# Q and K blocks of an encoder layer: fewer VectorE steps per block, and parts of Q, K and the gates emitted sooner

## The chip, the cores and the metric

The kernel runs on 1 core of one Trainium2 chip, as a single launch. The metric is the device time of that launch in microseconds (us). A core has one TensorE (PE), which multiplies matrices, and VectorE (DVE), ScalarE (ACT), GpSimd (POOL) and SyncE (SP), each with an instruction queue of its own that is worked off in order. The engines wait for each other through semaphores.

## The reference, cut to what matters

One encoder layer on a sequence of 1024 tokens of width 1024, fp32 in and out:

```python
u = rms_norm(x, norm1_g)
proj = u @ w_in                 # q | k | v | cb | cc | ch | ga | gb
q = rms_norm(q.reshape(B, S, 8, 64), q_norm_g)   # per head
k = rms_norm(k.reshape(B, S, 8, 64), k_norm_g)
y_a = neighbourhood_attention(q, k, v, rpb) @ w_attn_branch
y_b = short_gated_conv(cb, cc, ch, conv_w) @ w_conv_branch
merged = sigmoid(ga) * y_a + sigmoid(gb) * y_b
x = x + merged @ w_o
x = x + square(relu(rms_norm(x, norm2_g) @ w_mlp_in)) @ w_mlp_out

def rms_norm(x, g):
    return x * rsqrt(mean(x * x, axis=-1) + EPS) * g
```

q, k and v are 512 wide, and so are the convolution's cb, cc and ch; the gates ga and gb are 1024 wide each. The change touches the norm of q and k and what is emitted around it.

## The kernel before, in words

**Precision.** TensorE multiplies in fp16, with every fp32 operand split into a high part (its fp16 copy) and a low part (the value less that copy). Three passes (high by high, high by low, low by high) make up a product. A product of 1024 deep is therefore 24 matmuls of 128x128 by 128x512. The function `unit` emits these and adds one to a counter of units.

**Weights.** A piece of weights (the class `Chunk`) is loaded as raw fp32 in four parts by SyncE. Its `prep` squares the parts on ScalarE (L266), adds the sums on VectorE (L270, L272), adds over the partitions with a matmul by ones (L201), and from that makes a power of two as the scale. Then ScalarE writes the high parts (L306) and VectorE the low parts (L297). After each pair of low parts, SyncE is given the next load (`load_upto`): there are five raw buffers.

**Order.** The order of instructions on each engine is written out by hand, as the order of emission. Work beside the matmuls stands in Python generators of which every `yield` ends a step. Those in `fg` are advanced by `step`, those in `bg` (weights, first come first served) by `tick`. `unit(mms, post, steps, ticks)` emits a product, then what was put off until the product was emitted, and then so many steps and ticks. A generator that has to stand back until a unit count is reached does so by `apart`.

**The stage of the change.** After norm 1 (`norm`; ScalarE, GpSimd and VectorE) and its transposes by DMA (`turn_row`), the V units follow, then eight units of Q (rows in the order 2, 6, 3, 7, 4, 5, 0, 1), eight units of K, the first chunk of the convolution in two halves, and then the attention. Beside the Q units also run: `sforms`, which turns rows of the normed input into the gates' sums and differences (rows scaled on ScalarE at L484, four GpSimd instructions per pair of rows at L490, high and low parts at L504 and L506, and a store). Its table SFORM gives at which unit count which pair is scaled and summed (last number 0) or split into its parts (1). K's weight parts are made beside the Q units, and those of the first convolution chunk beside the K units.

**One block of Q or K** (`qk_vec`): ScalarE moves the product out of its PSUM bank (L714, which is also when the bank is free) and squares it (L715). VectorE sums per head (L718). `rstd` makes the inverse root: a VectorE step that adds epsilon (L405), the root on ScalarE (L406), then four VectorE steps (L408 to L414) that refine it. K's result is then scaled once more (L722). VectorE multiplies the block by it (L725), and for K by the norm weights (L728). ScalarE copies the high part (L732) and VectorE writes the low part (L734). For Q both parts are written twice side by side (1024 wide). The result stands in one of two buffers, and `finish_qk`, three units later, transposes it by a DMA on SyncE's queue (L745). Q and K units take PSUM banks "d" and "o" by turns; there are three banks "d", three "s" and two "o". Both halves of the first convolution chunk take banks "o" (L794). The loop emits

```python
        unit(tok_mms(ps, actU, b, ch, 8, 512, 0), post, 4, 6 if 4 < n < 8 else 3)
```

that is, four steps and three or six ticks per block.

Of the kernel before, what the change touches and what calls it, by code (L numbers as in the profile page):

```python
# [21 lines left out]
HD = 64  # L22
# [30 lines left out]
def encoder_block(ctx: ExitStack, tc: tile.TileContext, x, weights, cols, gqk, rel, masks, out):  # L53
# [22 lines left out]
        return bank("dsodsods"[rc[0] % 8])  # L76


    sc = base.tile([128, 516], F32, name="sc")
    sci = sc.bitcast(I32)  # L80
    area = {"keep": [0, 0, 148], "prep": [148, 148, 244], "tmp": [244, 244, 516]}

    def cols_of(kind, n):
        a = area[kind]
# [6 lines left out]
    def keep(n=1):  # L91
        return cols_of("keep", n)

    def tmp(n=1):
        return cols_of("tmp", n)

    def at(c, i, n=1):
        return slice(c.start + i, c.start + i + n)

    def mul(a, b, out=None):  # L100
        out = out or tmp(a.stop - a.start)
        V.tensor_tensor(sc[:, out], sc[:, a], sc[:, b], op=OP.mult)
        return out
# [78 lines left out]
    def apart(mark, n=3, of=units):  # L182
        while of[0] < mark + n and not forced[0]:
            yield WAIT
# [37 lines left out]
    def settle():  # L222
        while late:
            late.pop(0)()
# [20 lines left out]
    class Chunk:  # L245
# [9 lines left out]
        def prep(self):  # L255
            n = len(self.widths)
            nk = sum(k for k, _ in self.widths)
            rm, a, b, s = (cols_of("prep", i) for i in (nk, 1, 1, 1))
            self.inv = keep()
            tot = sum(k * w for k, w in self.widths)  # L260
            if self.kind in "QKCG":
                self.parts = wsp.tile([128, 2, tot], F16, name="w16_ws", tag="ws")
                for p, (k, w) in enumerate(self.widths):
                    while len(self.raw) <= p:
                        yield WAIT
                    A.activation(self.parts[:, 1, :k * w].bitcast(BF16), self.raw[p][:, :k * w], AF.Square,  # L266
                                 accum_out=sc[:, at(rm, p)])
                    spend(0, 300 + k * w * 7 // 8)
                    yield
                V.tensor_reduce(sc[:, a], sc[:, at(rm, 0, n)], axis=AX, op=OP.add)  # L270
                c = ones_col()
                V.tensor_tensor(c, sc[:, a], sc[:, gm2], op=OP.mult)  # L272
                yield from apart(units[0], 1 if self.kind == "Q" else 3)
                yield from all_sum(c, b, bank(self.bank) if self.bank else anybank(), 1e-36, int(self.kind != "Q"))
                yield from pow2_half(b, 14, s, self.inv, more=self.more)
            else:
                yield from self.largest(rm, a, b)
                yield from pow2(b, 14, s, self.inv, False, more=self.more)
            V.tensor_scalar(sc[:, rm], sc[:, self.rows], sc[:, s], None, op0=OP.mult)  # L279
            yield  # L280
            while done[0] < self.first or self.tag not in wpool:
                yield WAIT
            if self.kind not in "QKCG":
                self.parts = wpool[self.tag].tile([128, 2, tot], F16, name="w16_" + self.tag, tag=self.tag)
            f = o = 0
            todo = []
            for p, (k, w) in enumerate(self.widths):
                todo.append((p, [(i * w, w, rm.start + o + i) for i in range(k)], f))
                f += k * w
                o += k  # L290
            prev = None
            for it in todo + [None]:
                if prev:
                    p, parts, f = prev
                    for o, m, c in parts:
                        hi, lo = (self.parts[:, w, f + o:f + o + m] for w in range(2))
                        V.scalar_tensor_tensor(lo, self.raw[p][:, o:o + m], sc[:, c:c + 1], hi,  # L297
                                               op0=OP.mult, op1=OP.subtract)
                    done[0] += 1
                    load_upto(done[0] + 5)  # L300
                    spend(sum(m + 130 for _, m, _ in parts))
                if it:
                    p, parts, f = it
                    spend(0, sum(m * 7 // 8 + 120 for _, m, _ in parts))
                    for o, m, c in parts:
                        A.activation(self.parts[:, 0, f + o:f + o + m], self.raw[p][:, o:o + m], AF.Copy,  # L306
                                     scale=sc[:, c:c + 1])
                prev = it
                self.split = it is None
                yield  # L310
# [81 lines left out]
    def gain(g, top, s, inv):  # L392
# [5 lines left out]
        yield  # L398
        yield from pow2(m, top, s, inv, floor=False)

    def rstd(ss, n, y, top):

        k = ss.stop - ss.start
        v, q = tmp(k), tmp(k)
        V.tensor_scalar(sc[:, v], sc[:, ss], 4.0 ** -top / n, 4.0 ** -top * EPS, op0=OP.mult, op1=OP.add)  # L405
        A.activation(sc[:, q], sc[:, v], AF.Sqrt)  # L406
        yield
        V.reciprocal(sc[:, y], sc[:, q])  # L408
        yield
        V.scalar_tensor_tensor(sc[:, q], sc[:, y], -0.5, sc[:, y], op0=OP.mult, op1=OP.mult)  # L410
        yield
        mul(q, v, q)
        yield
        V.scalar_tensor_tensor(sc[:, y], sc[:, q], 1.5, sc[:, y], op0=OP.add, op1=OP.mult)  # L414
        yield
# [20 lines left out]
    def norm(xin, sq, u, y, pool):  # L436

        ss = tmp()
        A.activation(sq, xin, AF.Square, accum_out=sc[:, ss])
        yield  # L440
        yield from rpow(ss, D, y, 9)
        if pool:
            G.tensor_scalar(u[:, 0], xin, sc[:, y], 1.0, op0=OP.mult, op1=OP.mult)
        else:
            A.activation(u[:, 0], xin, AF.Copy, scale=sc[:, y])
        yield
        V.scalar_tensor_tensor(u[:, 1], xin, sc[:, y], u[:, 0], op0=OP.mult, op1=OP.subtract)
# [25 lines left out]
    ys = keep(8)  # L473
    ORDER, BYPOOL = (2, 6, 3, 7, 4, 5, 0, 1), (4, 5)
    ln = [norm(xt[:, b], sq, u16[:, ORDER.index(b) % 4], at(ys, b), b in BYPOOL) for b in range(8)]
    GS = dram.tile([128, 4, 4, 2, 512], F16, name="gs")

    turned, formed = set(), [0]
    SFORM = ((9, 0, 0), (9, 2, 1), (10, 1, 0), (10, 3, 1), (11, 0, 1), (12, 1, 1))

    def sform_rows(n):
        assert n in turned and n + 4 in turned
# [31 lines left out]
    def ln_step(b, n=1):  # L514
        for _ in range(n):
            advance(ln[b])

    def qk_gain():
        g = gq[:, 0]
        V.tensor_tensor(g, g, gq[:, 1], op=OP.mult)  # L520
        yield
        yield from gain(g, 11, sgq, isgq)

    def turn_row(b):
        ln_turn(u16[:, ORDER.index(b) % 4], b, UT)
# [145 lines left out]
                v_post(b, j, s)  # L671
    v_unit(2, 0)
    settle()
    for b in 4, 5:
        ln_step(b)
        turn_row(b)
# [3 lines left out]
    tick(2)  # L680
    v_unit(6, 0)
    settle()
    tick()
    v_unit(3, 0)
    sform_rows(3)
    sform_sums(3)
    tick(2)
    v_unit(7, 1)
    for b in 0, 1:
        ln_step(b, 2)  # L690
        turn_row(b)
    fg.append(qk_gain())
    fg.append(sforms())
    for b in 4, 5:
        v_unit(b, 11)
# [15 lines left out]
    def qk_vec(ps, inv, kind, res):  # L711
        qs = wqk.tile([128, 512], F32, name="qs", bufs=3)
        sq = wqk.tile([128, 512], F32, name="sq", bufs=1)
        A.activation(qs, ps, AF.Copy, scale=sc[:, inv])  # L714
        A.activation(sq, qs, AF.Square)  # L715
        yield
        ss, y = tmp(8), tmp(8)
        V.tensor_reduce(sc[:, ss], sq.rearrange("p (h d) -> p h d", h=8), axis=AX, op=OP.add)  # L718
        yield
        yield from rstd(ss, HD, y, 12 if kind == "q" else 0)  # L720
        if kind == "k":
            V.tensor_scalar(sc[:, y], sc[:, y], sc[:, sgq], None, op0=OP.mult)  # L722
            yield
        q3 = qs.rearrange("p (h d) -> p h d", h=8)
        V.tensor_tensor(q3, q3, sc[:, y][:, :, None].to_broadcast([128, 8, HD]), op=OP.mult)  # L725
        yield
        if kind == "k":
            V.tensor_tensor(q3, q3, gq[:, 0][:, None, :].to_broadcast([128, 8, HD]), op=OP.mult)  # L728
        r = 2 if kind == "q" else 1
        t = wqk.tile([128, 8, 2, r, HD], F16, name=kind + "16", tag="q16")  # L730
        q4 = q3[:, :, None, :].to_broadcast([128, 8, r, HD])
        A.activation(t[:, :, 0], q4, AF.Copy)  # L732
        yield
        V.tensor_tensor(t[:, :, 1], q4, t[:, :, 0], op=OP.subtract)  # L734
        res.append(t)

    q16 = {}
# [9 lines left out]
    for n, (kind, b) in enumerate(todo):  # L747
# [5 lines left out]

        def post(ps=ps, kind=kind, n=n, ch=ch):
            fg.append(qk_vec(ps, ch.inv, kind, q16[n]))
        unit(tok_mms(ps, actU, b, ch, 8, 512, 0), post, 4, 6 if 4 < n < 8 else 3)
        if n == 3:
            forced[0] = True
            while formed[0] < 4:
# [31 lines left out]

    conv_start(0)
    push(cConv[1])
    first = [bank("o"), bank("o")]  # L794
    for half in range(2):
        unit(ch_mms(first[half], actU, half, cConv[0], 8, 384, 0), None, 8, 4)
        finish_qk(13 + half)
# [1124 lines left out]
```

## Time and profile before

| | before |
|---|---|
| time, median of 3 runs | 1205.65 us (1205.05 to 1205.97) |
| the profiled execution: its time | 1205.96 us |
| the profiled execution: its span | 1204.2 us |
| granted TensorE clock | 1.0 |
| PE busy | 1190.9 us (99%) |
| DVE busy | 929.0 us (77%) |
| ACT busy | 763.3 us (63%) |
| POOL busy | 435.1 us (36%) |

The span is what the profile shows from the first to the last instruction; the time of that execution is 1.8 us more. A row of a timeline begins with the start in us from the beginning of the span, then the length, the engine, the line of the program, the operation and what it writes and reads; in brackets stand the idle time ahead of it and who ended that. Rows of grouped lines give, after the shapes and the count, the busy time in us, the mean of one in ns, and the idle time ahead of them.

### The profile page before, as it was taken

The page shows a single profiled execution, that of the slowest core. Times are in us where ns is not written, and L with a number is a line of the kernel's source. Part 1 is how long each engine was busy: PE and PEld are TensorE (multiplying, and loading weights), DVE is VectorE, ACT ScalarE, POOL GpSimd, SP SyncE. Part 2 cuts the span into 40 slices and gives each one's busy share as a digit, 9 for nine tenths or more (in the row PEclk, how much of TensorE's full clock was granted, in tenths as well). Part 3 has the DMA queues.
Part 4 walks back from the last instruction along what each step waited for, and adds up shares of the span by engine and source line. Part 5 has one row for each costly group of instructions (what it writes and reads, how often), then busy time and mean ns, then how long its engine had stood idle before and what let it go on. Part 6 is the DMA issues. An engine that isn't in the chain of part 4 may idle for free.

```text
span 1204.2 us, 16886 instructions
## 1 busy us (share of the span) xinstructions
PE 1190.9 (99%) x6206; PEld 574.7 (48%) x6206; DVE 929.0 (77%) x1721; ACT 763.3 (63%) x1185; POOL 435.1 (36%) x292
## 2 busy tenths in 40 slices
PE   8999999999999999999999999999999999999998
PEld 6444445555444444444468444444444444444444
DVE  6767988988368686877878655545549999999997
ACT  7876679867554555337779778678676744746440
POOL 1641011222311112001004465565567471554662
PEclk9999999999999999999999999999999999999999
DMA  9956746676451211224286545445465926345302
GB/s 284 220 181 139 139 119 134 130 146 120 106 121 68 64 60 52 70 92 188 53 159 185 183 156 192 151 138 193 147 247 201 355 94 223 124 139 194 105 35 105
DMA packets 177250, 174.91 MB, mean 145 GB/s; under 512 B 137744, under 2 KB 138256, under 8 KB 173072
## 3 DMA queue, kind: packets, MB, share of 16 engines
q1 hardware_dynamic: 176592, 169.65, 49.0%
q10 hardware_dynamic: 576, 4.19, 0.8%
q8 instruction: 48, 0.79, 0.3%
q14 instruction: 34, 0.28, 0.1%
HBM read 102.51 MB, written 37.75 MB: 116 GB/s over the span
## 4 chain that ended last, share of the span: by engine, by line
PE 78%; DVE 5%; issue 1%; SPq 1%; ACT 1%; DMA 0%; DVEq 0%; ACTq 0%
PE ps_d L210 28%; PE ps_s L210 24%; PE ps_o L210 17%; PE ps_d L1017 6%; PE ps_o L994 1%; PE ps_s L937 1%; SPq L1088 1%; DVE P L977 1%; DVE w_s L1141 1%; DVE sz L951 1%; DVE sg L1257 0%; DVE w_ws L297 0%; ACT w_s L1145 0%; DMA uT<-gs 0%; DVE sc L317 0%
## 5 line engine op out<-in xcount | busy, mean ns | idle before, releaser
L210 PEld LDWEIGHTS <-ops 128*128 128x128 f16 x1356 | 132.5, 98 | 157.3
L210 PEld LDWEIGHTS <-w 128*128 128x128 f16 x1368 | 132.9, 98 | 139.4
L1017 PE MATMUL ps_d<-uT,w_ws 128*128 128x512 f16 x528 | 123.7, 379 | 0.1
L210 PE MATMUL ps_d<-ops 128*128 128x512 f16 (+1 forms) x528 | 118.3, 374 | 0.0
L1743 ACT ACTIVATE ops<-hf,sc 128x2048 f16<-128x2048 f32 x26 | 52.0, 2000 | 98.2 <-PE ps_o L210 35.5
L210 PE MATMUL ps_s<-ops 128*128 128x512 f16 x492 | 112.9, 379 | 0.0
L1130 POOL TENSOR_TENSOR tsum<-raw 128x512 f32<-128x512 f32 x28 | 46.3, 1668 | 148.8 <-ACT raw L1116 148.7
L1323 POOL TENSOR_TENSOR as<-as 128x512 f32<-128x512 f32 x56 | 77.5, 1385 | 38.9 <-ACT as L1603 35.6
L210 PEld LDWEIGHTS <-w_s 128*128 128x128 f16 x588 | 56.7, 98 | 69.6 <-DVE w_s L1141 1.5
L210 PEld LDWEIGHTS <-uT 128*128 128x128 f16 x528 | 51.4, 98 | 64.0 <-issue 2.3
L210 PE MATMUL ps_d<-u2x,w 128*128 128x512 f16 (+1 forms) x360 | 80.0, 372 | 0.0
L1017 PEld LDWEIGHTS <-w_ws 128*128 128x128 f16 x528 | 51.2, 98 | 54.5 <-DVE cv L839 0.4
L210 PE MATMUL ps_o<-ops 128*128 128x512 f16 x336 | 77.1, 379 | 0.0
L1745 DVE SCALAR_TENSOR_TENSOR ops<-hf,sc,ops 128x2048 f16<-128x2048 f32 x26 | 73.4, 2822 | 4.3 <-ACT ops L1743 4.2
L210 PE MATMUL ps_o<-u2T,w 128*128 128x512 f16 (+1 forms) x324 | 71.7, 371 | 0.0
L1116 ACT ACTIVATE raw<-raw,sc 128x256 f32<-128x256 f32 x172 | 71.0, 494 | 0.9 <-DMA raw<-in_weights 0.9
L1130 POOL TENSOR_TENSOR gsum<-raw 128x512 f32<-128x512 f32 x14 | 19.0, 1377 | 132.3 <-issue 71.3
L1145 ACT ACTIVATE w<-raw,sc 128x512 f16<-128x512 f32 (+1 forms) x28 | 24.6, 927 | 54.0 <-DVE sc L432 54.0
L210 PE MATMUL ps_s<-u2T,w 128*128 128x512 f16 (+1 forms) x252 | 52.7, 359 | 0.0
L1636 DVE TENSOR_TENSOR as<-ps_d,as 128x512 f32<-128x512 f32 (+1 forms) x14 | 9.4, 672 | 55.7 <-ACT as L1655 53.4
L960 ACT ACTIVATE sz<-sz,sc 128x384 f32<-128x384 f32 (+1 forms) x64 | 37.2, 582 | 22.4 <-DVE sc L951 15.0
L306 ACT ACTIVATE w_ws<-raw,sc 128x512 f16<-128x512 f32 (+2 forms) x72 | 40.8, 637 | 14.2 <-DVE sc L279 14.2
(360 smaller groups left out, 2633.5 us busy)
## 6 DMA issues: line engine op xcount, KB each, us to landing
raw<-in_weights SPq DMA_DIRECT2D x88, 512.0 KB, 5.3
hs<-as SPq DMA_DIRECT2D x16, 1792.0 KB, 8.8
hf<-hs SPq DMA_DIRECT2D x26, 1024.0 KB, 7.4
w2x<-in_weights SPq DMA_DIRECT2D x16, 512.0 KB, 8.6
raw<-in_weights SPq DMA_DIRECT2D x16, 384.0 KB, 3.4
xt<-in_x SPq DMA_DIRECT2D x8, 512.0 KB, 8.1
gs<-s ACTq DMA_DIRECT2D x4, 1024.0 KB, 3.9
x<-in_x SPq DMA_DIRECT2D x8, 512.0 KB, 10.1
```

The source lines that it names most:

```text
L210: T.matmul(ps, l, r, start=a, stop=b)
L306: A.activation(self.parts[:, 0, f + o:f + o + m], self.raw[p][:, o:o + m], AF.Copy, scale=sc[:, c:c + 1])
L937: T.matmul(ps[:, :nb * 128], QD[:, p, e, w, i * 128:(i + 1) * 128], KD[:, 2 * p + e, lo * 128:(lo + nb) * 128], start=w == 0, stop=w == 1)
L951: V.tensor_tensor_reduce(z[:, :d["n"]], d["ps"][:, :d["n"]], bm, sc[:, cneg], 3.0e38, OP.add, OP.min, accum_out=sc[:, d["mx"]])
L960: A.activation(z, z, AF.Exp, scale=-1.0, bias=sc[:, d["mx"]], accum_out=sc[:, d["sm"]])
L1017: T.matmul(ps, l, r, start=a, stop=b)
L1116: A.activation(v, v, AF.Copy, scale=sc[:, at(g, 4 * i + k)])
L1130: G.tensor_tensor(t[:, o], a, b, op=OP.add)
L1145: A.activation(o(0), w, AF.Copy, scale=sc[:, s])
L1323: sub.tensor_tensor(z[o], z[a], z[b], op=op)
L1743: A.activation(P[:, 1, 0], hf, AF.Copy, scale=sc[:, Rs])
L1745: V.scalar_tensor_tensor(P[:, 1, 1], hf, sc[:, Rs], P[:, 1, 0], op0=OP.mult, op1=OP.subtract)
```

## The change

- `rstd` adds epsilon as the bias of ScalarE's root, and scales there; the VectorE step L405 goes. Three kept columns (`guard`) hold the bias, written by GpSimd. The last steps are rewritten to the same value. `rstd` is also called in the second norm.
- The norm weights `gq` are multiplied by their scale once (`qk_gain`), so that K's step L722 goes.
- The low part of Q is computed once (512 wide) on VectorE, and ScalarE copies it to its second place.
- K's chunk puts its sum matmul two units after its squares, not three.
- In SFORM the sums of pair 1 come a unit sooner, at unit 9, ahead of the split of pair 2. Steps of norm 1 for rows 0 and 1, and their transposes, stand earlier among the V units. `qk_gain` stands ahead of V's unit 7, and that unit has ten ticks rather than one.
- Every unit of Q and K has six ticks; before, only those of n = 5, 6 and 7 had.
- The second half of the first convolution chunk takes a bank "s", not "o".

```diff
--- before.py
+++ after.py
@@ -76,9 +76,9 @@
         return bank("dsodsods"[rc[0] % 8])
 
 
-    sc = base.tile([128, 516], F32, name="sc")
+    sc = base.tile([128, 520], F32, name="sc")
     sci = sc.bitcast(I32)
-    area = {"keep": [0, 0, 148], "prep": [148, 148, 244], "tmp": [244, 244, 516]}
+    area = {"keep": [0, 0, 152], "prep": [152, 152, 248], "tmp": [248, 248, 520]}
 
     def cols_of(kind, n):
         a = area[kind]
@@ -270,7 +270,7 @@
                 V.tensor_reduce(sc[:, a], sc[:, at(rm, 0, n)], axis=AX, op=OP.add)
                 c = ones_col()
                 V.tensor_tensor(c, sc[:, a], sc[:, gm2], op=OP.mult)
-                yield from apart(units[0], 1 if self.kind == "Q" else 3)
+                yield from apart(units[0], {"Q": 1, "K": 2}.get(self.kind, 3))
                 yield from all_sum(c, b, bank(self.bank) if self.bank else anybank(), 1e-36, int(self.kind != "Q"))
                 yield from pow2_half(b, 14, s, self.inv, more=self.more)
             else:
@@ -398,18 +398,19 @@
         yield
         yield from pow2(m, top, s, inv, floor=False)
 
+    guard = {top: keep() for top in (12, 0, 9)}
+
     def rstd(ss, n, y, top):
 
         k = ss.stop - ss.start
-        v, q = tmp(k), tmp(k)
-        V.tensor_scalar(sc[:, v], sc[:, ss], 4.0 ** -top / n, 4.0 ** -top * EPS, op0=OP.mult, op1=OP.add)
-        A.activation(sc[:, q], sc[:, v], AF.Sqrt)
+        q, c = tmp(k), 4.0 ** -top / n
+        A.activation(sc[:, q], sc[:, ss], AF.Sqrt, scale=c, bias=sc[:, guard[top]])
         yield
         V.reciprocal(sc[:, y], sc[:, q])
         yield
-        V.scalar_tensor_tensor(sc[:, q], sc[:, y], -0.5, sc[:, y], op0=OP.mult, op1=OP.mult)
-        yield
-        mul(q, v, q)
+        V.scalar_tensor_tensor(sc[:, q], sc[:, y], -0.5 * c, sc[:, y], op0=OP.mult, op1=OP.mult)
+        yield
+        V.scalar_tensor_tensor(sc[:, q], sc[:, ss], n * EPS, sc[:, q], op0=OP.add, op1=OP.mult)
         yield
         V.scalar_tensor_tensor(sc[:, y], sc[:, q], 1.5, sc[:, y], op0=OP.add, op1=OP.mult)
         yield
@@ -473,10 +474,12 @@
     ys = keep(8)
     ORDER, BYPOOL = (2, 6, 3, 7, 4, 5, 0, 1), (4, 5)
     ln = [norm(xt[:, b], sq, u16[:, ORDER.index(b) % 4], at(ys, b), b in BYPOOL) for b in range(8)]
+    for top in guard:
+        G.memset(sc[:, guard[top]], 4.0 ** -top * EPS)
     GS = dram.tile([128, 4, 4, 2, 512], F16, name="gs")
 
     turned, formed = set(), [0]
-    SFORM = ((9, 0, 0), (9, 2, 1), (10, 1, 0), (10, 3, 1), (11, 0, 1), (12, 1, 1))
+    SFORM = ((9, 0, 0), (9, 1, 0), (9, 2, 1), (10, 3, 1), (11, 0, 1), (12, 1, 1))
 
     def sform_rows(n):
         assert n in turned and n + 4 in turned
@@ -520,6 +523,8 @@
         V.tensor_tensor(g, g, gq[:, 1], op=OP.mult)
         yield
         yield from gain(g, 11, sgq, isgq)
+        V.tensor_scalar(g, g, sc[:, sgq], None, op0=OP.mult)
+        yield
 
     def turn_row(b):
         ln_turn(u16[:, ORDER.index(b) % 4], b, UT)
@@ -671,6 +676,7 @@
                 v_post(b, j, s)
     v_unit(2, 0)
     settle()
+    ln_step(0)
     for b in 4, 5:
         ln_step(b)
         turn_row(b)
@@ -680,16 +686,19 @@
     tick(2)
     v_unit(6, 0)
     settle()
+    ln_step(0)
+    turn_row(0)
     tick()
+    ln_step(1)
     v_unit(3, 0)
+    tick()
+    ln_step(1)
+    turn_row(1)
+    tick()
     sform_rows(3)
     sform_sums(3)
-    tick(2)
-    v_unit(7, 1)
-    for b in 0, 1:
-        ln_step(b, 2)
-        turn_row(b)
     fg.append(qk_gain())
+    v_unit(7, 10)
     fg.append(sforms())
     for b in 4, 5:
         v_unit(b, 11)
@@ -718,9 +727,6 @@
         V.tensor_reduce(sc[:, ss], sq.rearrange("p (h d) -> p h d", h=8), axis=AX, op=OP.add)
         yield
         yield from rstd(ss, HD, y, 12 if kind == "q" else 0)
-        if kind == "k":
-            V.tensor_scalar(sc[:, y], sc[:, y], sc[:, sgq], None, op0=OP.mult)
-            yield
         q3 = qs.rearrange("p (h d) -> p h d", h=8)
         V.tensor_tensor(q3, q3, sc[:, y][:, :, None].to_broadcast([128, 8, HD]), op=OP.mult)
         yield
@@ -728,10 +734,12 @@
             V.tensor_tensor(q3, q3, gq[:, 0][:, None, :].to_broadcast([128, 8, HD]), op=OP.mult)
         r = 2 if kind == "q" else 1
         t = wqk.tile([128, 8, 2, r, HD], F16, name=kind + "16", tag="q16")
-        q4 = q3[:, :, None, :].to_broadcast([128, 8, r, HD])
-        A.activation(t[:, :, 0], q4, AF.Copy)
-        yield
-        V.tensor_tensor(t[:, :, 1], q4, t[:, :, 0], op=OP.subtract)
+        A.activation(t[:, :, 0], q3[:, :, None, :].to_broadcast([128, 8, r, HD]), AF.Copy)
+        yield
+        V.tensor_tensor(t[:, :, 1, 0], q3, t[:, :, 0, 0], op=OP.subtract)
+        if r == 2:
+            yield
+            A.activation(t[:, :, 1, 1], t[:, :, 1, 0], AF.Copy)
         res.append(t)
 
     q16 = {}
@@ -753,7 +761,7 @@
 
         def post(ps=ps, kind=kind, n=n, ch=ch):
             fg.append(qk_vec(ps, ch.inv, kind, q16[n]))
-        unit(tok_mms(ps, actU, b, ch, 8, 512, 0), post, 4, 6 if 4 < n < 8 else 3)
+        unit(tok_mms(ps, actU, b, ch, 8, 512, 0), post, 4, 6)
         if n == 3:
             forced[0] = True
             while formed[0] < 4:
@@ -791,7 +799,7 @@
 
     conv_start(0)
     push(cConv[1])
-    first = [bank("o"), bank("o")]
+    first = [bank("o"), bank("s")]
     for half in range(2):
         unit(ch_mms(first[half], actU, half, cConv[0], 8, 384, 0), None, 8, 4)
         finish_qk(13 + half)
```

## The prediction

> **What bounds the kernel now.** I read the page's engine line first, then the list of waits for TensorE, then the timeline of TensorE over the stage that the change touches.
>
> ```profile
> span 1204.2 us, 16886 instructions
> PE 1190.9 (99%) x6206; PEld 574.7 (48%) x6206; DVE 929.0 (77%) x1721; ACT 763.3 (63%) x1185; POOL 435.1 (36%) x292
> ...
> PE ps_d L210 <- DVE w_ws L297: 1.5, 2, 0.9
> PE ps_o L210 <- ACT qs L714: 1.3, 1, 1.3
> ...
> PE ps_d L201 <- DVE ones L272: 0.4, 1, 0.4
> ...
> 71.35 5.34 PE L210 MATMUL ps_o<-w_ws,uT 128*128 128x512 f16 x24
> ...
> 97.28 0.38 PE L210 MATMUL ps_d<-w_ws,uT 128*128 128x512 f16 x1
> 98.60 2.94 PE L210 MATMUL ps_d<-w_ws,uT 128*128 128x512 f16 x12 [0.95 <-DVE w_ws L297]
> ...
> 140.77 5.55 PE L210 MATMUL ps_o<-uT,w_ws 128*128 128x512 f16 x24
> 147.65 5.34 PE L210 MATMUL ps_o<-uT,w_ws 128*128 128x512 f16 x24 [1.33 <-ACT qs L714]
> 153.43 0.16 PE L201 MATMUL ps_d<-ones 128*128 128x1 bf16 x1 [0.44 <-DVE ones L272]
> ```
>
> TensorE is busy 99% of the span, so the change can win only what TensorE waits, and lose whatever new wait it makes. I number the blocks by their order: Q0 to Q7, then K0 to K7, then the first convolution chunk in two halves. A unit of 24 matmuls steps on by (97.28 - 71.35) / 5 = 5.19 us. From K0 at 97.28, ten units without a wait would bring the second chunk's sum (L201) to 97.28 + 51.9 = 149.2; it stands at 153.43. The list of waits names three: K's low parts (1.5), the second half's bank, which K7's eviction (L714) frees (1.3), and that sum's input (0.4). Between 3.2 us (the list's idle time) and 4.2 us (the delay on the grid) is all that this stage has to give.
>
> So the question is when ScalarE and VectorE, which run behind TensorE here, are done with K5 (the change leaves the first half in the bank that K5's eviction frees), and when the second chunk's sum is ready.
>
> **The removed VectorE steps.** By the grouped lines of this stage:
>
> ```profile
> L734 DVE TENSOR_TENSOR q<-qs,q 128x1024 f16<-128x1024 f32 x8 | 9.8, 1223 | 9.1 <-ACT q L732 9.1
> L734 DVE TENSOR_TENSOR k<-qs,k 128x512 f16<-128x512 f32 x8 | 5.5, 690 | 2.0 <-ACT k L732 1.9
> L405 DVE TENSOR_SCALAR sc<-sc 128x8 f32<-128x8 f32 x16 | 2.7, 167 | 0.0
> L722 DVE TENSOR_SCALAR sc<-sc 128x8 f32<-128x8 f32 x8 | 1.8, 226 | 0.0
> ```
>
> Gone are 16 x 0.167 (epsilon, L405) and 8 x 0.226 (K's scale, L722), and the 8 subtractions of Q halve from 1.223 to about 0.69, K's form: 2.7 + 1.8 + 4.3 = 8.8 us of VectorE. ScalarE gets 8 copies of 128x512 for Q's repeated low part; no row shows that form, and between nothing hidden and all of it on the path lie 0 and 8 x 0.63 us, 0.63 being K's copy L732 (below). I take 0: the copy stands after the next square, while ScalarE waits for VectorE. In the norm of the MLP one such step less per call lies under a busy TensorE: 0 (at most 5 x 0.167 gained). Three GpSimd memsets stand at the start, where GpSimd idles: 0.
>
> A step less in a generator also moves everything behind it, and that is where I see the cost.
>
> **K's weight parts come two blocks sooner.**
>
> ```profile
> 74.06 1.91 ACT L504 ACTIVATE s<-xt 128x2048 f16<-128x2048 f32 x1 [3.20 <-POOL xt L490]
> 77.12 1.04 ACT L266 ACTIVATE w_ws<-raw 128x1024 bf16<-128x1024 f32 x1
> 83.53 0.67 ACT L714 ACTIVATE qs<-ps_d,sc 128x512 f32<-128x512 f32 x1
> 87.38 0.67 ACT L714 ACTIVATE qs<-ps_o,sc 128x512 f32<-128x512 f32 x1
> 96.38 2.54 ACT L306 ACTIVATE w_ws<-raw,sc 128x512 f16<-128x512 f32 x4
> 111.69 1.06 ACT L732 ACTIVATE q<-qs 128x1024 f16<-128x1024 f32 x1 [4.08 <-DMA qD<-q]
> 117.61 0.67 ACT L714 ACTIVATE qs<-ps_d,sc 128x512 f32<-128x512 f32 x1
> ```
>
> The Q loop goes on at 87.38 - 83.53 = 3.85 us per block. Its start moves up by some 2.2 us: GpSimd's last sums begin about 1.8 sooner (their rows are scaled right after Q's parts), and K's fourth square, 1.04 at 77.12, now runs ahead of the gates' last copy, where ScalarE idles 3.20. Bounds 0 and 3.2. K's parts now follow Q3 instead of Q5: L306 starts at 96.38 - 2.2 - 2 x 3.85 = 86.5, less or more, and the parts are done near 93.3. K0 needs them from 97.28: the 1.5 us wait is gone, with 4 us to spare.
>
> K's sum on TensorE also goes two units forward, to just before Q3 (71.35). By the same reckoning its input is ready about 70.9; half a microsecond later and TensorE waits there. That costs nothing in the end as long as a later wait is longer, which is the next point.
>
> **Q1's transpose now waits behind the loads.** SyncE's queue:
>
> ```profile
> 99.24 5.12 SPq L234 DMA_DIRECT2D raw<-in_weights  x4
> 104.41 10.94 SPq L745 DMA_TRANSPOSE qD<-q  x3
> ...
> DMA to landing us min/median/max: 3.1/4.3/7.2
> ```
>
> Before, the four loads of the convolution, each waiting for a pair of K's low parts, stood between Q2's and Q3's transposes; Q3's landed at 111.6, after 7.2 us, and Q5's copy waited 4.08 us for its buffer. Now they stand right behind Q0's transpose, so that Q1's waits, and Q3's copy for that: 111.69 - 10.75 = 100.9 (10.75 is 2.2 + 2 x 3.85 and 0.85 for the bias step that no longer stands among the parts). If it landed in the median 4.3 it would be 2.9 sooner. Evictions then: Q5 101.9, Q6 105.7, Q7 109.5. K0's has four squares of the convolution ahead of it and comes at about 115.9, where before it was 117.61.
>
> **K's loop gets longer.** This is the term that decides.
>
> ```profile
> 123.31 0.69 DVE L718 TENSOR_REDUCE sc<-sq 128x8 f32<-128x512 f32 x1
> 123.92 0.15 DVE L414 SCALAR_TENSOR_TENSOR sc<-sc 128x8 f32<-128x8 f32 x1
> 124.60 0.64 DVE L725 TENSOR_TENSOR qs<-qs,sc 128x512 f32<-128x512 f32 x1
> 125.27 0.69 DVE L728 TENSOR_TENSOR qs<-qs,gq 128x512 f32<-128x512 f32 x1
> ...
> 124.36 0.67 ACT L714 ACTIVATE qs<-ps_d,sc 128x512 f32<-128x512 f32 x1
> 125.06 0.63 ACT L715 ACTIVATE sq<-qs 128x512 f32<-128x512 f32 x1
> 126.00 0.63 ACT L732 ACTIVATE k<-qs 128x512 f16<-128x512 f32 x1 [0.31 <-DVE qs L728]
> 127.66 0.67 ACT L714 ACTIVATE qs<-ps_o,sc 128x512 f32<-128x512 f32 x1
> ...
> 146.39 0.63 ACT L732 ACTIVATE k<-qs 128x512 f16<-128x512 f32 x1 [2.42 <-DVE qs L728]
> 146.93 0.67 ACT L714 ACTIVATE qs<-ps_o,sc 128x512 f32<-128x512 f32 x1
> 147.63 0.63 ACT L715 ACTIVATE sq<-qs 128x512 f32<-128x512 f32 x1
> 148.17 0.83 ACT L266 ACTIVATE w_ws<-raw 128x768 bf16<-128x768 f32 x1
> 150.05 0.63 ACT L732 ACTIVATE k<-qs 128x512 f16<-128x512 f32 x1
> ```
>
> Here the evictions are 127.66 - 124.36 = 3.30 apart: ScalarE evicts and squares the block two ahead before it copies (L732) this one, and VectorE never runs dry. In the changed order, with L722's step gone, the copy of K(n) stands ahead of the eviction of K(n+2). So one round becomes a single chain: reduce 0.61 to the next start, L414 0.18, L725 0.67, L728 0.73, copy to eviction 0.54, eviction to square 0.70, square 0.65, and the next reduce: 4.08 us. From K0 at 115.9: K1 119.7 (a Q copy is still in that round), K2 123.8, K3 127.9, K4 132.6 with 0.6 for the convolution's scale steps.
>
> ```profile
> L297 DVE SCALAR_TENSOR_TENSOR w_ws<-raw,sc,w_ws 128x384 f16<-128x384 f32 x8 | 4.5, 605 | 0.0
> ```
>
> The first chunk's parts, which stood behind K6's eviction, now stand behind K4's, ahead of K5's: 4.5 us busy, some 4.2 of it added to that round. K5 is evicted at 132.6 + 4.1 + 4.2 = 140.9 to 141.6. TensorE wants that bank at 97.28 + 41.5 = 138.8 and waits 2.8: the first half starts at 141.6, where before it was 140.77. The new bank for the second half saves nothing beyond that.
>
> Then K4's copy waits for K2's transpose, queued behind four more loads (0 to 2; I take 0.9, as the last load lands about then): K6 145.9, K7 150.0, before 146.93. From K7's eviction to the sum's input it was 6.5 us (146.93 to 153.43). Now K6's copy stands behind all four squares and the sum behind K7's two products: 0.70 + 0.54 + two pairs of squares of 1.88 (148.17 to 150.05), a root 0.1, copy 0.63, subtract 0.69, small steps 0.35, 0.69 + 0.70, sum 0.35 = 8.5. So L201 comes at 158.4, 4.9 us later than 153.43. TensorE would have been there at 141.6 + 10.4 = 152.0, so earlier TensorE waits of up to 6 us change nothing.
>
> After that the order is the old one. The profiled run took 1205.96 us for its span of 1204.2 (0.31 over the median); 4.9 us on the median of 1205.65 gives 1210.5.
>
> [...]
>
> ```profile
> 125.00:150.00 25.00, 23.64 (x110) 10.50 (x109) 24.03 (x77) 17.16 (x35) 0.00 (x0) 1.00 0.70 140
> ```
>
> In this stretch VectorE is busy 24.03 of 25 us and ScalarE 17.16. [...] My sum says that the load falls and the order, not the load, takes over.
>
> **Rivals.**
> 1. Faster: VectorE's 8.8 us are what held the stage, and evictions keep up. For it: VectorE's 24.03 of 25. Against it: the chain of 4.08 us, whose links are all in the queues. Its place is K5's eviction; it decides if that ends before 138.8 and the second sum's input is there by 149.2, some 9 us sooner than I have it. TensorE then loses its three waits: 1205.65 - 3.2 = 1202.4. Chance 0.12.
> 2. A draw: Q1's transpose lands in the median 4.3 us (2.9 sooner), K2's is not late (0.9), and the start is at its bound (1.0 sooner). 4.9 - 4.8 = +0.1: 1205.8. For it: each has a row. Against it: all three are needed, and the loads have the same spacing as when the 7.2 was seen. Chance 0.11.
> 3. Forecast: 0.77, own range 1208.0 to 1213.0 (the transpose's 2.9 sooner gives +2.0; K2's at 2 and the start at its old time give +8.2, of which I leave the last microsecond out).
>
> **The numbers.** A change of 0.2% is 2.4 us, about what can be told from none. Slower: the forecast, less a twentieth of its weight near +2: 0.75. Same: 0.13, faster: 0.12. For 8 in 10 the range reaches down to the draw, 1205.5, and up to 1212.8.
>
> **What the profile would show.** Right: no TensorE wait on L297 at K0; ScalarE idle for some 5.8 us near 95 to 101 ended by DMA qD<-q; K's evictions 4.1 apart; TensorE waiting on ScalarE's eviction at the first convolution half and several microseconds on L272 before the first attention scores. Wrong: K's evictions still 3.3 apart, or L201 before 153.

## The result, and the profile after

| | before | after |
|---|---|---|
| median | 1204.87 us (1204.07 to 1205.97, 6 runs) | 1211.96 us (1211.41 to 1214.76, 6 runs) |
| ratio to before | | 1.0061 (95% interval 1.0049 to 1.0074) |
| the profiled execution: time, span | 1205.96, 1204.2 | 1211.41, 1209.6 |

The change makes the kernel 7.1 us slower (1211.96 - 1204.87). The page's engine line and the list of waits for TensorE after the change (engine, tile and line, what was waited for: us in total, times, longest):

```profile
span 1209.6 us, 16867 instructions
PE 1191.7 (99%) x6206; PEld 574.5 (47%) x6206; DVE 922.4 (76%) x1693; ACT 769.6 (64%) x1193; POOL 431.5 (36%) x295
...
PE ps_d L201 <- DVE ones L272: 4.5, 1, 4.5
PE ps_o L210 <- ACT qs L723: 3.2, 1, 3.2
```

VectorE has 6.6 us less work (929.0 to 922.4) and ScalarE 6.3 more. K0's wait for low parts (1.5 us) is gone. In its place two longer waits have grown: the first convolution half waits for K5's eviction (L723, which was L714), and the second chunk's sum (L201) for VectorE. TensorE's timeline shows both, and something behind each:

```profile
96.50 5.34 PE L210 MATMUL ps_d<-w_ws,uT 128*128 128x512 f16 x24
...
132.78 5.34 PE L210 MATMUL ps_o<-w_ws,uT 128*128 128x512 f16 x24
141.36 7.03 PE L210 MATMUL ps_o<-uT,w_ws 128*128 128x512 f16 x24 [3.24 <-ACT qs L723]
148.22 5.34 PE L210 MATMUL ps_s<-uT,w_ws 128*128 128x512 f16 x24
158.07 0.16 PE L201 MATMUL ps_d<-ones 128*128 128x1 bf16 x1 [4.50 <-DVE ones L272]
158.17 0.38 PE L945 MATMUL ps_s<-kD,qD 128*128 128x256 f16 x2
158.39 3.09 PE L1025 MATMUL ps_d<-uT,w_ws 128*128 128x512 f16 x7
```

The same 24 matmuls take 7.03 us after the wait of 3.24 and 5.34 elsewhere; the seven behind the second wait take 3.09, where seven took 1.67 before. Measured from Q0's start (54.63 here, 55.81 before), L201 comes at 158.07 - 54.63 = 103.44 us, before at 153.43 - 55.81 = 97.62.

The windows of the two stretches show the same in the granted TensorE clock. A row gives the stretch and its length, then the busy time of PE, PEld, DVE, ACT and POOL with the instructions of each in brackets, then that clock, the DMA engines' share and GB/s:

```profile
125.00:150.00 25.00, 21.76 (x94) 9.45 (x93) 19.29 (x55) 13.64 (x27) 0.00 (x0) 0.93 0.52 117
150.00:175.00 25.00, 20.50 (x94) 9.46 (x93) 19.48 (x63) 19.69 (x44) 0.13 (x2) 0.93 0.47 122
```

The clock is 0.93 in both, where before it was 1.00. And no engine is full: VectorE is busy 19.29 of 25 us (24.03 before), ScalarE 13.64 (17.16 before). They wait for each other. ScalarE's timeline says how (L723 evicts, L737 copies, numbers in brackets are its idle time):

```profile
99.25 1.06 ACT L737 ACTIVATE q<-qs 128x1024 f16<-128x1024 f32 x1 [4.15 <-DMA qD<-q]
...
108.19 1.06 ACT L737 ACTIVATE q<-qs 128x1024 f16<-128x1024 f32 x1 [1.74 <-DMA qD<-q]
...
115.63 0.67 ACT L723 ACTIVATE qs<-ps_d,sc 128x512 f32<-128x512 f32 x1
...
123.09 0.63 ACT L737 ACTIVATE k<-qs 128x512 f16<-128x512 f32 x1 [1.22 <-DVE qs L734]
123.63 0.67 ACT L723 ACTIVATE qs<-ps_d,sc 128x512 f32<-128x512 f32 x1
...
127.24 0.63 ACT L737 ACTIVATE k<-qs 128x512 f16<-128x512 f32 x1 [1.22 <-DVE qs L734]
127.77 0.67 ACT L723 ACTIVATE qs<-ps_o,sc 128x512 f32<-128x512 f32 x1
...
140.64 0.67 ACT L723 ACTIVATE qs<-ps_o,sc 128x512 f32<-128x512 f32 x1
...
149.67 0.67 ACT L723 ACTIVATE qs<-ps_o,sc 128x512 f32<-128x512 f32 x1
```

In the two rounds shown each copy of K waits 1.22 us for VectorE's product, and the next eviction stands behind the copy: 127.77 - 123.63 = 4.14 us per block, where it was 3.30. VectorE's side of the same round, from its timeline:

```profile
124.99 0.69 DVE L727 TENSOR_REDUCE sc<-sq 128x8 f32<-128x512 f32 x1 [0.47 <-ACT sq L724]
...
127.90 0.69 DVE L739 TENSOR_TENSOR k<-qs,k 128x512 f16<-128x512 f32 x1 [0.55 <-ACT k L737]
```

VectorE now runs dry twice per round; before, its rows of the K rounds had no gap up to 147 us. The two waits for transposes at the head of ScalarE's rows above (4.15 and 1.74 us) come from SyncE's queue, where the loads now stand ahead of seven transposes:

```profile
88.33 5.05 SPq L234 DMA_DIRECT2D raw<-in_weights  x4
93.43 29.85 SPq L753 DMA_TRANSPOSE qD<-q  x7
```

### The profile page after: what moved, and what is told of

It is laid out like the page before. It is cut to its first block, busy times and chain, and to the rows that moved or that the text cites. A ratio compares the mean times of both kernels' runs of the same rounds, so it can differ in the third digit from the quotient of the medians.

```text
span 1209.6 us, 16867 instructions
## 1 busy us (share of the span) xinstructions
PE 1191.7 (99%) x6206; PEld 574.5 (47%) x6206; DVE 922.4 (76%) x1693; ACT 769.6 (64%) x1193; POOL 431.5 (36%) x295
## 4 chain that ended last, share of the span: by engine, by line
PE 81%; DVE 7%; ACT 6%; DMA 2%; issue 2%; POOL 1%; SPq 0%; DVEq 0%; ACTq 0%; POOLq 0%
PE ps_d L210 28%; PE ps_s L210 25%; PE ps_o L210 17%; PE ps_d L1025 8%; PE ps_s L945 1%; POOL xt L493 1%; PE ps_o L1002 1%; DVE w_ws L297 1%; DMA qD<-q 1%; DVE w_s L1149 1%; ACT w_ws L266 1%; ACT qs L723 1%; DMA uT<-u 1%; DVE qs L731 1%; DVE sc L727 1%
```

## The experiments

The theory was that the order is the cost, by two edits: K's generator has one step less, so that each K block becomes one chain through both engines; and the loads of the convolution's weights stand ahead of transposes that ScalarE waits for. The main rivals were that VectorE's load, the added copies on ScalarE, or slow transposes as such set the time. This table holds all runs. The last two columns are worked out from TensorE's timeline of each run: L201's start less Q0's start, and the start of the tenth pair of score matmuls less Q0's start (170.06 - 55.81 for before).

| run | median, us | against before on the same chip (its median) | ratio, 95% interval | Q0 to L201 | Q0 to tenth score |
|---|---|---|---|---|---|
| before | | | | 97.62 | 114.25 |
| after | 1211.96 | +7.1 (1204.87) | 1.0061 (1.0049 to 1.0074) | 103.44 | 121.53 |
| lost_step_alone | 1210.52 | +5.8 (1204.69) | 1.0043 (1.0029 to 1.0057) | 104.17 | 120.58 |
| k_step | 1203.11 | -1.9 (1205.00) | 0.9986 (0.9977 to 0.9994) | 95.67 | 112.30 |
| late_loads | 1207.89 | +2.9 (1205.00) | 1.0024 (1.0015 to 1.0033) | 99.35 | 117.20 |
| k_step_late_loads | 1200.47 | -4.5 (1205.00) | 0.9959 (0.9946 to 0.9973) | 93.52 | 109.85 |
| steps_only | 1202.34 | -2.7 (1205.00) | 0.9980 (0.9972 to 0.9989) | 96.27 | 112.91 |
| order_only | 1203.97 | -0.7 (1204.69) | 0.9994 (0.9985 to 1.0002) | 95.74 | 113.83 |
| order_late_loads | 1201.92 | -2.9 (1204.77) | 0.9978 (0.9968 to 0.9987) | 94.82 | 111.45 |
| copy_twice | 1213.73 | +9.0 (1204.69) | 1.0074 (1.0061 to 1.0086) | 104.31 | 123.07 |
| fill_wait | 1212.71 | +8.0 (1204.69) | 1.0064 (1.0051 to 1.0077) | 104.20 | 120.53 |
| fill_wait_2 | 1211.46 | +6.7 (1204.77) | 1.0059 (1.0047 to 1.0072) | 103.48 | 119.82 |

The last column less 114.25 follows the third within 1.4 us, but for the first fill_wait: the time is won and lost in this stage.

**The step, put back.** K's generator gets an empty step where the scale step stood.

```diff
         yield from rstd(ss, HD, y, 12 if kind == "q" else 0)
+        if kind == "k":
+            yield
```

> The changed kernel with one empty step put back in K's generator where the scale step L722 stood; no work is added, only ScalarE's and VectorE's order in the K loop is again that of before (eviction of K(n+2) ahead of the copy of K(n)). Theory (the lost step made each K round one chain of 4.15 us): K's evictions come 2.9 to 3.3 us apart, K5's ends before 138, the first convolution half starts without a wait at 138, the second chunk's sum (L201) comes near 151 where it came at 158.07; 1203.5 us (1202 to 1205.5). Rival (the loads ahead of the transposes, and the added copies on ScalarE, are what holds the loop): evictions stay 4.1 apart, L201 stays near 158, 1211 to 1212.5 us.

It took 1203.11 us. ScalarE's timeline has the evictions 3.10 and 2.93 apart, and they wait for a small VectorE step (L415) rather than for the copy:

```profile
121.34 0.67 ACT L723 ACTIVATE qs<-ps_d,sc 128x512 f32<-128x512 f32 x1
...
124.44 0.69 ACT L723 ACTIVATE qs<-ps_o,sc 128x512 f32<-128x512 f32 x1 [0.47 <-DVE sc L415]
...
127.37 0.69 ACT L723 ACTIVATE qs<-ps_d,sc 128x512 f32<-128x512 f32 x1 [0.47 <-DVE sc L415]
```

An empty step, without any work in it, is worth 8.9 us (1211.96 - 1203.11), more than the 7.1 that the change lost.

**The step, taken out of the kernel before.** The reverse: the old arithmetic and order, with one step boundary less.

```diff
             V.tensor_scalar(sc[:, y], sc[:, y], sc[:, sgq], None, op0=OP.mult)
-            yield
```

> The kernel before with nothing changed but one yield: the step boundary behind L722 is taken out, so that K's generator has one step less, as in the changed kernel, while all arithmetic and every other mark stay. Theory (the lost step boundary alone makes the K round one chain): K's evictions are 4.3 to 4.4 us apart where they were 3.30 (L722 is now a link of the chain), K7's eviction comes near 152, the second chunk's sum (L201) at 159 to 161; 1212.5 us (1209.5 to 1215). Rival (VectorE's work sets the round): same work, so 3.3 apart and 1204 to 1206 us.

It took 1210.52 us, with K's evictions 4.42 and 4.41 apart (126.07 - 121.65, 130.48 - 126.07), by ScalarE's timeline:

```profile
121.65 0.67 ACT L714 ACTIVATE qs<-ps_o,sc 128x512 f32<-128x512 f32 x1
...
126.07 0.67 ACT L714 ACTIVATE qs<-ps_d,sc 128x512 f32<-128x512 f32 x1
...
130.48 0.67 ACT L714 ACTIVATE qs<-ps_o,sc 128x512 f32<-128x512 f32 x1
```

VectorE has the same instructions as before, and the kernel loses 5.8 us. That VectorE's amount of work sets the round, whatever the order, is ruled out. TensorE's wait stands at another place here, at the first half, since the convolution's parts are emitted later in this order:

```profile
145.88 13.08 PE L210 MATMUL ps_o<-uT,w_ws 128*128 128x512 f16 x48 [5.24 <-ACT w_ws L306]
```

**The loads, moved behind the transposes.** The first chunk's four loads are held until Q3's transpose is issued, the second's until K3's.

```diff
+        if n in (3, 11):
+            held[0] = 100
         unit(tok_mms(ps, actU, b, ch, 8, 512, 0), post, 4, 6)
...
+        if n in (6, 14):
+            held[0] = 0
+            load_upto(done[0] + 5)
```

> The changed kernel with SyncE's order alone altered: the four raw loads of the first convolution chunk stand behind Q3's transpose rather than ahead of Q1's, and those of the second chunk behind K3's rather than ahead of K2's; the other engines keep their order. Theory (transposes are late because they queue behind loads that wait): ScalarE's waits for a transpose (4.15, 1.74 and 1.89 us) go, K's evictions stay 4.15 apart but start 5.9 sooner, the first half doesn't wait, L201 comes at 158.07 - 7.8 = 150.3; 1203.5 us (1202 to 1205.5). Rival (a transpose takes 7 us here whatever stands ahead of it): the waits stay over 3 us in sum, L201 after 155; 1209 to 1212.5 us.

> Both of the two edits. Theory: no wait of TensorE over 0.3 us is left between the first Q block and the attention; L201 at 148 to 149; 1201 us (1200 to 1202.5), below the kernel before by its three waits there of 1.97, 1.49 and 0.6 us. Rival (ScalarE's eight added copies or VectorE's load hold the stage next): L201 at 151 or later, 1203 to 1206 us.

Alone it took 1207.89 us. The waits of 4.15, 1.74 and 1.89 us went, but Q6's copy then waited 1.53 for Q4's transpose, which now stands behind the loads, and the sum's wait stayed (ScalarE's timeline, then TensorE's):

```profile
111.35 1.06 ACT L737 ACTIVATE q<-qs 128x1024 f16<-128x1024 f32 x1 [1.53 <-DMA qD<-q]
```

```profile
154.07 0.16 PE L201 MATMUL ps_d<-ones 128*128 128x1 bf16 x1 [5.51 <-DVE ones L272]
```

K7's eviction came 4.0 us sooner (145.68 where it was 149.67) and L201 with it; I had expected 7.8, the sum of the waits, as if none would come up at the next block. So in the changed kernel the place of the loads costs 4.1 us (1211.96 - 1207.89), and my price of it was nearly twice too high. This is not a share of the 7.1 that the change lost. The kernel before has a wait of 4.08 us for a transpose too, with K's step in place the same move gains 2.6 us (1203.11 - 1200.47), and `order_only` below, with the loads in their new place and the step kept, is not slower than before. How much worse the new place of the loads is than the old one, no run isolates. Both edits together took 1200.47 us, as expected, and no wait is left for TensorE in the stage:

```profile
143.06 5.34 PE L210 MATMUL ps_s<-uT,w_ws 128*128 128x512 f16 x24
148.24 0.17 PE L201 MATMUL ps_d<-ones 128*128 128x1 bf16 x1
```

This version beats both kernels, the one before by 4.5 us.

**Arithmetic and order apart.** `steps_only` is the kernel before with the fewer VectorE steps and an empty step for K; `order_only` is the kernel before with the new marks, ticks and bank alone; `order_late_loads` is the latter with the loads moved.

> The kernel before with the fewer VectorE steps alone (epsilon in the root, weights scaled once, Q's low part once and copied on ScalarE), an empty step kept for K, and the order of emission of before. Theory (the arithmetic is harmless and the order is the cost): K0's wait for L297 stays at 1.5 to 2.0 us, the waits for the second half's bank and for L201 shrink from 2.1 to 0 to 1; 1203.5 us (1202.5 to 1205). Rival (the eight copies on ScalarE cost what they take): slower than before by 2 to 5 us, 1207 to 1210.

> The kernel before with the new order alone (marks, ticks, SFORM, rows 0 and 1, the bank of the second half) and all VectorE steps of before, so that K keeps its step. Theory: ScalarE's order is that of the run with K's empty step, VectorE's K round is 3.3 us rather than 3.0; K0's wait for L297 is gone, L201 waits some 2 us more than there; L201 about 97.5 us behind Q0's start (97.62 before); 1205 us (1203.5 to 1206.5). Rival (the sooner emission is itself harmful): 1207 to 1212.

> The new order with all VectorE steps of before (so K keeps its step), and the raw loads behind Q3's and K3's transposes as in the run with late loads. Theory (with the order right, the fewer VectorE steps are worth next to nothing, since TensorE waits for nothing there): K's evictions 3.3 us apart, L201 waits 0 to 0.6 us, 1200.8 us (1200 to 1202), no more than 0.5 from the same with the fewer steps (1200.5). Rival (VectorE's load was what held the stage): L201 waits 1.5 us or more, 1202.5 to 1204.5 us.

The arithmetic alone gains 2.7 us, 1.2 more than I expected. The order alone, with K's step kept, is not told from before (0.9985 to 1.0002): K0's wait goes, and the sum waits 1.91. With the loads moved, the fewer steps make 1201.92 into 1200.47. I had expected no more than 0.5 there and the rival 2 or more; the truth lies between, the sum still waiting 1.03 us without them. The intervals of the two just overlap.

**ScalarE's copies.** In the changed kernel the copy of Q's low part is issued twice.

```diff
             A.activation(t[:, :, 1, 1], t[:, :, 1, 0], AF.Copy)
+            A.activation(t[:, :, 1, 1], t[:, :, 1, 0], AF.Copy)
```

> The changed kernel with ScalarE's copy of Q's low part issued twice, eight more copies of 0.61 us. Theory (these copies lie where ScalarE waits for VectorE, so I set them at nothing): 1212 to 1213.3 us, evictions of Q still 3.85 apart. Rival (each copy is on the path): 8 x 0.61 = 4.9 us more, 1216 to 1217.5.

1213.73 us: 1.8 more, neither 0 nor 4.9. Q2's and Q3's evictions stay 3.86 and 3.91 apart (76.93, 80.79, 84.70). K0's comes 7.14 behind Q7's (109.44 to 116.58) where it was 6.48 (109.15 to 115.63): there the copy stands between the convolution's squares, and ScalarE has no idle time to hide it. L201 comes 0.87 later behind Q0 (104.31 - 103.44), and the slow matmuls behind it add 0.67 by the tenth score (123.07 - 121.53 is 1.54). The run tests a second copy, not the first, whose place is the same.

**The slow matmuls.** TensorE's wait for L201 is filled with matmuls into a bank that nothing reads.

```diff
+    extra = [bank("d") for _ in range(3)][0]
+    for i in range(17):
+        T.matmul(extra, UT[:, 0, 0][:, 0:128], UT[:, 0, 1][:, 0:512], start=i == 0, stop=i == 16)
     while not q16[15]:
```

> The changed kernel with 20 matmuls of 128x512 into a bank that nothing reads, put where TensorE waits 4.5 us for the second chunk's sum. They take 4.3 us and take nothing away. Theory (after an idle of over 3 us TensorE runs matmuls at half speed, 0.427 in place of 0.216 us each, for about 3 us): the sum stays at 103.4 behind Q0's start, the slow steps behind it go; 1.4 us less, 1210.6 us (1209.8 to 1211.4). Rival (the slow steps have another cause in the start of the attention): they stay, 1211.8 to 1213 us.

> As the run with matmuls in the wait, with 17 of them, which end ahead of the sum's input, and with the rotation of the banks left as it is in the changed kernel (there it had moved by one, and a wait of 0.9 us near 625 us came of it). Theory (TensorE's half speed follows an idle): the sum 103.4 to 103.9 us behind Q0's start, no slow steps behind it, the wait near 625 us gone, 1210.8 us (1210.0 to 1211.6). Rival (the matmuls cost as much as they save): 1212 to 1213 us.

The first form, with 20 matmuls and one bank, took 1212.71 us: the slow steps behind the sum went, but the matmuls ended after the sum was ready, and the shifted banks brought a wait of 0.9 us in a later stage. The second form:

```profile
155.65 3.83 PE L808 MATMUL ps_d<-uT 128*128 128x512 f16 x17
159.31 0.17 PE L201 MATMUL ps_d<-ones 128*128 128x1 bf16 x1
159.34 0.38 PE L948 MATMUL ps_s<-kD,qD 128*128 128x256 f16 x2
159.56 1.67 PE L1028 MATMUL ps_d<-uT,w_ws 128*128 128x512 f16 x7
```

The sum comes at 103.48, as in the changed kernel (its input was ready some 0.4 us sooner, at 158.92, so that 17 matmuls are still a little too long), and the seven matmuls behind it take 1.67 us rather than 3.09. From Q0 to the tenth score it is 119.82, 1.71 less. The time is 1211.46, 0.5 less by the medians: within what was expected, but the intervals of the two ratios overlap, so that the gain in time is shown by the trace of the stage alone.

## Why the prediction was right, and where it was off

**The weight parts: right.** K's high parts began at 86.15 (forecast 86.5), the low parts ended at 93.0 (93.3), and K0's wait went. K's sum, two units sooner, waited 0.24 us and cost nothing, since later waits were longer.

**Q1's transpose: right in kind, off in size.** ScalarE waited 4.15 us for it, not 5.8, and the copy came at 99.25, not 100.9. A wait of 1.74 for Q3's transpose, which I had not seen, came on top, and so K0's eviction stood at 115.63 (115.9) after all. Two errors cancelled.

**K's loop: right.** Forecast 4.08 us per block, measured 4.14. K5's eviction came at 140.64 (140.9 to 141.6), the first half at 141.36 (141.6), K7 at 149.67 (150.0), L201 at 158.07 (158.4). `lost_step_alone` and `k_step` show the cause: the eviction behind the copy, by one step boundary.

**The copies at nothing: not quite.** By `copy_twice`, where ScalarE waited for VectorE a copy cost nothing (Q2's and Q3's evictions 3.86 and 3.91 apart); at K0, among the squares, one cost its 0.6 (7.14 for 6.48).

**VectorE's saving: 6.6 us, not 8.8.** The page has 929.0 before and 922.4 after. The forecast left out the scaling of the norm weights that the change adds, one instruction of 1.3 us (L526); the rest is not worked out here. The forecast doesn't hang on it, since the chain and not VectorE's load sets the round in the changed order.

**The total: too small, 4.9 for 7.1.** One term was missing and one was too large. Missing is the half speed behind a wait: I priced a wait by its idle time alone, and behind L201 there were 1.4 us more (3.09 - 1.67). Behind the first half it was 1.7 (7.03 - 5.34), which the wait for the sum swallowed. The other comes of measuring on the grid of one execution. Q0 started at 55.81 there; in `steps_only` and `lost_step_alone`, with the same order up to that point, it started at 53.76 and 55.05. Counted from Q0, L201 is late by 5.8 us, not by the 4.6 that the grid shows (158.07 - 153.43). 5.8 and 1.4 make 7.2.

The term that the grid made too large is the head start of 2.2 us, with which the Q loop was to begin sooner. ScalarE's timelines, first before, then after:

```profile
75.88 0.67 ACT L714 ACTIVATE qs<-ps_d,sc 128x512 f32<-128x512 f32 x1
...
73.70 0.67 ACT L723 ACTIVATE qs<-ps_d,sc 128x512 f32<-128x512 f32 x1
```

On the span's grid Q0's eviction moved by 2.18 us, as forecast. Counted from Q0's start it moved by 1.00 (75.88 - 55.81 = 20.07, 73.70 - 54.63 = 19.07). The runs agree: 18.90 to 19.07 us in all nine with the new order, 20.07 to 20.53 in the three with the old. The other 1.18 us are the later start of Q0 in that one execution of before, and such starts differ by some 2 us from execution to execution with either order (54.06 to 55.83 with the new). So the places above that agree with the forecast to some 0.4 us do so in part by luck, since all of them stand on the span's grid. The profiled execution of before also took 1205.96 us, 1.1 over the median of the six.

**The rivals.** The faster one had the right mechanism for another kernel: with the K step kept, VectorE's load does set the round (3.30 us before, where VectorE was busy 24.03 of 25 us, and some 3.0 in `k_step`), and `steps_only` is 2.7 us faster. In that run (0.9980) the order of emission was held and a copy went from VectorE to ScalarE; but it also drops VectorE steps outright, so it doesn't show what the move alone is worth. The draw needed the transposes to be 2.9 us sooner; they were 1.65 sooner and then 1.74 late.

## What to carry to other kernels

In a kernel whose order is emitted from generators, a step boundary is part of the schedule: when an operation is taken out, leave its empty step in place (worth 8.9 us in the changed kernel) or redo the order, and look first at which instruction now stands ahead of each eviction. A load that waits for a buffer should not be queued ahead of a transfer that a busy engine waits for (4.1 us here, by `late_loads`). Price a wait of TensorE by what comes behind it as well (1.4 us here, behind L201), and lengths within a stage from the stage's own start, not from the span's.

## What was not expected of the hardware

Behind two waits of the changed kernel TensorE ran at half its clock for some microseconds; behind the first its granted clock was 0.50 or 0.51 in every stretch from 141.4 to 144.8 us. The windows show the granted clock, which stands behind the figures of the five engines: first the three microseconds behind the waits of 3.24 and 4.50 us in the changed kernel, then, in the kernel before, those behind the second chunk's sum:

```profile
141.40:144.40 3.00, 3.00 (x8) 1.08 (x8) 2.39 (x8) 0.87 (x2) 0.00 (x0) 0.50 1.13 249
158.20:161.20 3.00, 3.00 (x10) 1.17 (x10) 2.28 (x14) 2.63 (x5) 0.00 (x0) 0.55 0.43 79
...
153.50:156.50 3.00, 3.00 (x17) 1.58 (x17) 2.17 (x12) 2.13 (x4) 0.13 (x2) 1.00 0.16 30
```

At the full clock (1.00) a 128x512 matmul was issued every 0.216 us (5.18 / 24), and the 1.69 us lost behind the first wait (7.03 - 5.34) are eight times 0.211, as if eight matmuls took twice as long. The loss was 1.4 to 2.9 us, after waits of 3.17 to 5.51 us, and it doesn't follow their length: 24 matmuls behind a wait of 3.24 us lost 1.69, and the same 24 behind 3.17 us in `fill_wait_2` lost 2.94 (8.28 - 5.34). Once half speed also came after 1.91 us (`order_only`), but not after 1.82 (`k_step`). The timelines of TensorE, first of `order_only`:

```profile
151.42 0.16 PE L201 MATMUL ps_d<-ones 128*128 128x1 bf16 x1 [1.91 <-DVE ones L272]
151.53 0.38 PE L941 MATMUL ps_s<-kD,qD 128*128 128x256 f16 x2
151.74 3.08 PE L1021 MATMUL ps_d<-uT,w_ws 128*128 128x512 f16 x7
```

and of `k_step`:

```profile
149.73 0.16 PE L201 MATMUL ps_d<-ones 128*128 128x1 bf16 x1 [1.82 <-DVE ones L272]
149.83 0.38 PE L947 MATMUL ps_s<-kD,qD 128*128 128x256 f16 x2
150.04 1.67 PE L1027 MATMUL ps_d<-uT,w_ws 128*128 128x512 f16 x7
```

The trace shows the half (0.50, and 0.216 + 0.211 us per matmul). The "over 3 us" in what was expected of `fill_wait` fitted the waits of 3.24 and 4.50 us seen until then, but it is no bound: in `order_only` half speed came after a wait of 1.91 us, and behind the 4.49 us that TensorE of the kernel before waits for its first input the clock is 1.00 in every stretch up to 12 us. What decides when half speed begins, no run here settles.
